# Recurrent scan: the products of keys and values written in other hops of the plan

## The chip, the cores and the metric

One core of one Trainium2 chip. The metric is the time on the device for one execution, in microseconds (us); lower is better. Engines are named as the profile names them: PE is TensorE's matmul side and PEld its weight load, DVE is VectorE, ACT is ScalarE, POOL is GpSimd, and SP is the engine that issues most DMAs.

## The reference, cut to what matters

The program is a two-layer transformer on 256 latent and 256 context tokens of width 1024. Layer 0 mixes tokens with a bidirectional RWKV-7 recurrence, layer 1 with global attention, and feed-forward halves stand around both. The change touches only the recurrence, which is, for each of 16 heads and both directions:

```python
def rwkv_scan(state0, dd, reverse):
    def step(s, inp):
        r_t, w_t, k_t, v_t, a_t, b_t = inp
        sa = jnp.einsum('bhvk,bhk->bhv', s, a_t)
        s = s * w_t[:, :, None, :] + sa[..., None] * b_t[:, :, None, :] + v_t[..., None] * k_t[:, :, None, :]
        return s, jnp.einsum('bhvk,bhk->bhv', s, r_t)
```

Its result goes through a normalization by head, a gain, a bonus term and a gate, and then a projection. The change computes the same numbers.

## The kernel before, in words

The kernel runs its stages one after the other: feed-forward, the projections of the recurrence, `rwkv_scan`, then layer 0's end and layer 1. `rwkv_scan` handles **8 channel tiles** of 128 channels (two heads each). A tile has 8 chunks of 64 tokens in both directions at once, in two halves (hf 0 and 1) of four chunks.

For each tile four generators write its instructions:

- `produce` makes what doesn't depend on the state. A piece is named by a letter and digits. `s` pieces are the scores (four matmuls each, `scp`, L953; DVE masks them into `sc`, L958). `k` pieces transpose the keys of one half and one head (eight transposes, `btp`, L997; ACT copies them to `bkt` one hop later, L999). `v` pieces center the values of one half and one direction (eight matmuls, `vtp`, L977); after the second direction of a half, two ACT copies (L982, L983) put both into `uv` one hop later. So k01 is half 0, head 1, and v10 is half 1, direction 0.
- `solve` inverts small triangular blocks, nearly all on DVE (L1013 to L1035).
- `couple` joins the blocks with 32 by 32 matmuls (`cpl`, L1055, L1076, L1093) and ends with a row of ACT copies into `qt` and `tt` (L1081, L1085, L1098).
- `scan` is the chain. Each chunk takes three **hops**. Hop one: PE `rp` (L1173 and, with the state, L1180), ACT copies it to `rt` (L1184). Hop two: PE `up` from `rt` (L1191), ACT writes `uv` (L1193, L1194). Hop three: PE `sp` (L1200, L1207), ACT writes the new state `S` (L1212). The outputs `yp` (L1155, L1218) stand behind. Each hop needs the ACT copy of the hop before it.

A `readout` runs beside it: a squared copy `sqr` (L1238), small sums `ss` (L1246), and a transposed broadcast `bc` (L1260).

The order is written out by hand: the scheduler is switched off (`manual_schedule`), each engine runs its queue in program order, and `self.plan` says in which hop what is written. The period is P=24 hops: a new tile starts every 24 hops. I count hops 0 to 23 within a period. Tile c's pieces are written in hops 0 to 23 of its own period by `FILL`, `couple` in hops 3 to 16 of the next period, and its chain from hop 17 of that period to hop 16 of the one after. So the **first hop of a tile's chain is hop 17**, and in one period run: the chain of one tile, the couple of the next, the pieces of the one after. Within a hop the chain's part is written first, then what was left over from the hop before (the late copies), couple, the pieces of `FILL`, and the loads. So a piece of hop h stands on PE between the chain's part of hop h and that of hop h+1.

`BK` and `V` say in which hop the loads of the next tile's keys and values are written (SP's queue); they reuse the buffers that the pieces read. The tiles that share PSUM banks (`scp`, `vtp`, `btp`, `cpl`, `ss`, `bc`) rotate over five banks, so a piece that is written elsewhere also reuses another bank. `uv` has four buffers; POOL clears half of each (L971) in the hop of the first value piece of a half, in its queue among the DMAs that load the chain's operands (L929, L933) and the readout's (L1234, L1236).

Of the kernel before, what the change touches and what calls it, by code (L numbers as in the profile page):

```python
# [87 lines left out]
class Net:  # L88


    def __init__(self, ctx, tc, a):
        self.ctx, self.tc, self.nc, self.a = ctx, tc, tc.nc, a
        self.last = {}
        self.plan = dict(
            P=24, SOLVE=14, RATE=5, COUPLE=range(27, 41), SCAN=41,
            FILL={0: ("s000", "s001"), 1: ("s010",), 2: ("s011",), 3: ("s100", "s101"), 4: ("s110",), 5: ("s111",), 7: ("k00",),
                  8: ("k01",), 9: ("v00",), 11: ("v01",), 16: ("k10",), 19: ("k11",), 20: ("v10",), 21: ("v11",)},
            END={(0, 0): (5, (3, 3)), (0, 1): (5, (3, 3)), (1, 0): (5, (3, 3))}, WO=(4, 4), NI=(5, 5),
            FST=(1, 3), WAIT=16, RH=0, FB=16, CLEAR=(14, 18), AS=1, AR=(3, 6), BK=(9, 20), V=(12, 22), LOADS=(30, 42), SS=(6, 18), BC=(10, 22))
        nc = self.nc  # L100
        self.res = ctx.enter_context(tc.tile_pool(name="res", bufs=1))
        self.dram = ctx.enter_context(tc.tile_pool(name="dram", bufs=1, space=DRAM))
        self.vec = self.res.tile([128, NV, KT], F32, name="vec")
        self.cst = self.res.tile([128, NC], F32, name="cst")
        self.ones = self.res.tile([128, 128], F32, name="ones")
        cv = self.res.tile([128, KT, 2], F32, name="cv")
        self.cs = self.res.tile([128, KT, 32], F32, name="cs")
        self.mod = [self.res.tile([128, NMOD, KT, 2], F32, name=f"mod{l}") for l in range(2)]
        self.epsn = self.res.tile([128, 1], F32, name="epsn")
        self.epsg = self.res.tile([128, 1], F32, name="epsg")  # L110
        self.xsp = self.dram.tile([128, 2, KT, CTX], F32, name="xsp")
        nc.sync.dma_start(out=cv, in_=a["cv"])
        nc.sync.dma_start(out=self.vec, in_=a["vec"])
        nc.sync.dma_start(out=self.cst, in_=a["cst"])
        nc.vector.memset(self.epsg, GN_EPS)
        nc.vector.memset(self.ones, 1.0)
        nc.vector.memset(self.epsn, EPS)
        nc.vector.memset(self.cs, 0.0)
        nc.scalar.activation(out=self.cs[:, :, 0:2], in_=cv, func=AF.Silu)
# [19 lines left out]
    def mods01(self, b):  # L139
# [3 lines left out]
        for k4 in range(4):  # L143
            pool = self.first if k4 in self.plan["FST"] else self.wraw
            w = pool.tile([128, 2, 4, 128], F32, tag="mw" if pool is self.first else "raw", name="mw")
# [1473 lines left out]
```

## Time and profile before

| what | us |
|---|---|
| median of 3 runs | 2373.27 |
| the 3 runs | 2365.45, 2373.27, 2374.57 |
| the profiled execution, its own time | 2365.84 |
| its span in the profile | 2363.3 |
| `rwkv_scan` within the span | about 744 to 1116 |
| of that, the chain of the 8 tiles (first `rt` to last `yp`) | 794.9 to 1115 |
| PE busy, share of the span | 93% |
| mean granted TensorE clock | 0.947 |

The profile's times count from the start of the span. A granted clock of 1.00 is 2.4 GHz and 0.50 is 1.2 GHz. The trace counts a matmul of four-byte numbers as two instructions and a transpose as one, so that a value piece is x16 in it and a key piece x8. "busy" of PE counts a matmul to its modelled end; the distance from one start to the next tells better what an instruction costs.

### The profile page before, as it was taken

The page shows a single profiled execution, that of the slowest core. Times are in us where ns is not written, and L with a number is a line of the kernel's source. Part 1 is how long each engine was busy: PE and PEld are TensorE (multiplying, and loading weights), DVE is VectorE, ACT ScalarE, POOL GpSimd, SP SyncE. Part 2 cuts the span into 40 slices and gives each one's busy share as a digit, 9 for nine tenths or more (in the row PEclk, how much of TensorE's full clock was granted, in tenths as well). Part 3 has the DMA queues.
Part 4 walks back from the last instruction along what each step waited for, and adds up shares of the span by engine and source line. Part 5 has one row for each costly group of instructions (what it writes and reads, how often), then busy time and mean ns, then how long its engine had stood idle before and what let it go on. Part 6 is the DMA issues. An engine that isn't in the chain of part 4 may idle for free.

```text
span 2363.3 us, 44881 instructions
## 1 busy us (share of the span) xinstructions
PE 2200.9 (93%) x18548; PEld 1883.3 (80%) x18548; DVE 1516.0 (64%) x2609; ACT 1074.0 (45%) x1912; POOL 153.7 (7%) x222
## 2 busy tenths in 40 slices
PE   6999999887996899998999999999999999998998
PEld 4777889666765778776988788998878898678997
DVE  3798325576897666573788832479983367775554
ACT  3322225455884354454662222464232365554443
POOL 0000000000453122121000000000000000000000
PEclk9999999898998788988999999999999999798999
DMA  7577336442677433322567633567763364103654
GB/s 252 192 219 229 96 103 191 159 134 73 230 245 252 117 99 112 105 85 81 162 210 238 192 93 96 159 195 232 231 205 96 114 178 134 54 17 118 182 180 139
DMA packets 104860, 366.26 MB, mean 155 GB/s; under 512 B 13904, under 2 KB 16208, under 8 KB 101968
## 3 DMA queue, kind: packets, MB, share of 16 engines
q1 hardware_dynamic: 92880, 319.28, 43.2%
q0 software_dynamic: 11776, 44.12, 6.0%
q8 instruction: 145, 2.38, 0.4%
q14 instruction: 59, 0.48, 0.1%
HBM read 330.78 MB, written 32.57 MB: 154 GB/s over the span
## 4 chain that ended last, share of the span: by engine, by line
PE 51%; DVE 10%; ACT 6%; issue 5%; DMA 5%; POOL 1%; DVEq 0%; ACTq 0%; POOLq 0%
PE h L262 6%; PE h L260 5%; PE h L261 5%; PE yps L262 4%; PE yps L260 4%; PE yps L261 4%; DMA y<-in_modt 3%; DVE junk L214 3%; DVE wlo L253 2%; PE scp L953 1%; PE cpl L1055 1%; PE op L1483 1%; PE sp L1207 1%; PE up L1191 1%; PE vtp L977 1%
## 5 line engine op out<-in xcount | busy, mean ns | idle before, releaser
L252 ACT ACTIVATE whi<-wp 128x1024 fp32r<-128x1024 f32 (+1 forms) x396 | 409.3, 1034 | 742.7 <-PE h L261 396.0
L253 DVE TENSOR_TENSOR wlo<-wp,whi 128x1024 fp32r<-128x1024 f32 (+1 forms) x396 | 471.5, 1191 | 385.1 <-ACT whi L252 382.0
L262 PE MATMUL h<-nh,wlo 128*128 128x512 f32 (+1 forms) x1520 | 525.9, 347 | 16.5 <-DVE wlo L253 16.4
L260 PE MATMUL h<-nh,whi 128*128 128x512 f32 (+1 forms) x1520 | 524.5, 346 | 8.4 <-ACT whi L252 6.8
L261 PE MATMUL h<-nh,whi 128*128 128x512 f32 (+1 forms) x1520 | 523.4, 345 | 0.0
L262 PEld LDWEIGHTS h<-nh,wlo 128*128 128x128 f32 x1520 | 290.8, 192 | 59.7 <-DVE wlo L253 26.3
L260 PEld LDWEIGHTS h<-nh,whi 128*128 128x128 f32 x1520 | 291.2, 192 | 42.6 <-ACT whi L252 8.5
L261 PEld LDWEIGHTS h<-nh,whi 128*128 128x128 f32 x1520 | 291.1, 192 | 33.7
L262 PE MATMUL yps<-hid,wlo 128*128 128x256 f32 (+1 forms) x1034 | 314.2, 304 | 1.8 <-DVE wlo L253 1.8
L260 PE MATMUL yps<-hid,whi 128*128 128x256 f32 (+1 forms) x1034 | 314.2, 304 | 0.0
L261 PE MATMUL yps<-hid,whi 128*128 128x256 f32 (+1 forms) x1034 | 313.9, 304 | 0.0
L262 PEld LDWEIGHTS yps<-hid,wlo 128*128 128x128 f32 x1034 | 197.5, 191 | 10.5 <-DVE wlo L253 2.7
L261 PEld LDWEIGHTS yps<-hid,whi 128*128 128x128 f32 x1034 | 197.5, 191 | 7.9
L260 PEld LDWEIGHTS yps<-hid,whi 128*128 128x128 f32 x1034 | 197.5, 191 | 7.9
L214 DVE SCALAR_TENSOR_TENSOR junk<-y 128x1024 bf16<-128x1024 f32 x144 | 175.9, 1222 | 17.9 <-DMA y<-in_modt 15.8
L405 DVE TENSOR_TENSOR gg<-s,h 128x512 f32<-128x512 f32 (+1 forms) x98 | 55.9, 571 | 95.2 <-PE h L262 93.1
L214 DVE SCALAR_TENSOR_TENSOR junk<-dw,cb 128x1024 bf16<-128x1024 f32 x80 | 97.8, 1223 | 13.3 <-DMA dw<-in_modt 9.7
L407 ACT ACTIVATE hid<-gg 128x512 fp32r<-128x512 f32 (+1 forms) x98 | 52.4, 534 | 107.8 <-DVE gg L405 107.6
L262 PE MATMUL pp<-hid,wlo 128*128 128x512 f32 x232 | 92.3, 399 | 6.1 <-DVE wlo L253 6.0
L260 PE MATMUL pp<-hid,whi 128*128 128x512 f32 x232 | 92.6, 399 | 5.0 <-ACT whi L252 5.0
L261 PE MATMUL pp<-hid,whi 128*128 128x512 f32 x232 | 91.5, 395 | 0.0
L953 PE MATMUL scp<-ar,bk 64*128 64x128 f32 x512 | 45.4, 312 | 19.3 <-DVE G L334 11.6
(301 smaller groups left out, 3515.0 us busy)
## 6 DMA issues: line engine op xcount, KB each, us to landing
wp<-in_w SPq DMA_DIRECT2D x243, 512.0 KB, 3.6
wp<-in_w SPq DMA_DIRECT2D x94, 448.0 KB, 3.4
y<-in_modt SPq DMA_DIRECT2D x72, 512.0 KB, 4.4
dw<-in_modt SPq DMA_DIRECT2D x40, 512.0 KB, 4.3
wp<-in_wrkv SPq DMA_DIRECT2D x40, 512.0 KB, 4.0
mw<-in_modw SPq DMA_DIRECT2D x32, 512.0 KB, 5.1
far<-ar POOLq DMA_DIRECT2D x8, 1024.0 KB, 5.8
ar<-far SPq DMA_DIRECT2D x16, 512.0 KB, 4.8
```

Source lines behind the costliest of these rows:

```text
L214: nc.vector.scalar_tensor_tensor(out=junk, in0=ws[i % len(ws)], scalar=1.0, in1=cb[:, s], op0=ALU.mult, op1=ALU.mult, accum_out=self.mod[l ...
L252: nc.scalar.activation(out=hi, in_=raw, func=AF.Copy)
L253: nc.vector.tensor_tensor(out=lo, in0=raw, in1=hi.bitcast(F32), op=ALU.subtract)
L260: nc.tensor.matmul(out=ps, lhsT=wh, rhs=vh, start=first and j == 0, stop=False)
L261: nc.tensor.matmul(out=ps, lhsT=wh, rhs=vl, start=False, stop=False)
L262: nc.tensor.matmul(out=ps, lhsT=wl, rhs=vh, start=False, stop=last and j == n - 1)
L405: nc.vector.tensor_tensor(out=gg, in0=s1, in1=ps[1], op=ALU.mult)
L407: nc.scalar.activation(out=hi, in_=gg, func=AF.Copy)
L953: nc.tensor.matmul(out=p[h][:, c], lhsT=bk[q:q + 64, d, c], rhs=ar[q:q + 64, d, c].rearrange("p s i -> p (s i)"), start=True, stop=True, t ...
L977: nc.tensor.matmul(out=pv[q:q + 64, d, c], lhsT=v[:, d, c], rhs=cst[:, C_CE + q:C_CE + q + 64], start=True, stop=True, tile_position=(0, q))
L1055: nc.tensor.matmul(out=p[hf][q:q + 32, u], lhsT=lhs(8 * hf + u, q), rhs=rhs[q:q + 32, 8 * hf + u], start=True, stop=True, tile_position=(q ...
L1191: nc.tensor.matmul(out=p[w:w + 64, d], lhsT=tt[:, d, c, w:w + 64], rhs=rt[:, d], start=True, stop=True, tile_position=(0, w))
```

## The change

Two lines of the plan. The scores stay in hops 0 to 5. Of keys and values, by hop:

| hop | 7 | 8 | 9 | 11 | 16 | 17 | 19 | 20 | 21 | 23 |
|---|---|---|---|---|---|---|---|---|---|---|
| before | k00 | k01 | v00 | v01 | k10 | | k11 | v10 | v11 | |
| after | k00 | | k01 | | k10 | v10 | v11 | v00 | k11 | v01 |

```diff
             FILL={0: ("s000", "s001"), 1: ("s010",), 2: ("s011",), 3: ("s100", "s101"), 4: ("s110",), 5: ("s111",), 7: ("k00",),
-                  8: ("k01",), 9: ("v00",), 11: ("v01",), 16: ("k10",), 19: ("k11",), 20: ("v10",), 21: ("v11",)},
+                  9: ("k01",), 16: ("k10",), 17: ("v10",), 19: ("v11",), 20: ("v00",), 21: ("k11",), 23: ("v01",)},
-            FST=(1, 3), WAIT=16, RH=0, FB=16, CLEAR=(14, 18), AS=1, AR=(3, 6), BK=(9, 20), V=(12, 22), LOADS=(30, 42), SS=(6, 18), BC=(10, 22))
+            FST=(1, 3), WAIT=16, RH=0, FB=16, CLEAR=(14, 18), AS=1, AR=(3, 6), BK=(10, 22), V=(24, 20), LOADS=(30, 42), SS=(6, 18), BC=(10, 22))
```

The loads move with the pieces that free their buffers: the keys' by one and two hops, the values' of half 0 to the first hop of the next period and of half 1 to hop 20. SP's queue keeps its sequence of keys, values, keys, values.

On PE, hops 8 to 10 of a period (a number of matmuls is given once, as x8; the lines with a sign are what left and what came):

```order
 L1155 MATMUL yp<-r,S 64x64 x4
 L1055 MATMUL cpl<-td,qt 32x32 x16
-L997 MATMUL btp<-cst,bk 128x64 x8
 L1191 MATMUL up<-rt,tt 64x64 x4
 L1055 MATMUL cpl<-td,qt 32x32 x16
-L977 MATMUL vtp<-cst,v 64x64 x8
+L997 MATMUL btp<-cst,bk 128x64 x8
 L1200 MATMUL sp<-S,cst 64x128 x2
 L1207 MATMUL sp<-uv,bkt 64x64 x4
```

The transposes of k01 leave the place ahead of `up` and take that of the values v00 ahead of `sp`; two hops later v01 leaves in the same way.

On PE, hops 16 to 20, where a tile's chain begins:

```order
 L997 MATMUL btp<-cst,bk 128x64 x8
 L1173 MATMUL rp<-uv,sc 64x64 x4
+L977 MATMUL vtp<-cst,v 64x64 x8
 L1191 MATMUL up<-rt,tt 64x64 x4
 L1246 MATMUL ss<-cst,sqr 128x2 x4
 L1207 MATMUL sp<-uv,bkt 64x64 x4
 L1218 MATMUL yp<-sc,uv 64x64 x4
-L997 MATMUL btp<-cst,bk 128x64 x8
+L977 MATMUL vtp<-cst,v 64x64 x8
 L1173 MATMUL rp<-uv,sc 64x64 x4
 L1180 MATMUL rp<-S,ax 64x64 x4
```

The values v10 come between `rp` and `up` of the chain's first hop, and v11 take the place of the keys k11.

On ACT, hops 12 to 14 before (two copies of values, then the state, then couple's copies):

```order
530 L1194 ACTIVATE uv<-up 64x2x64
531 L982 ACTIVATE uv<-vtp 64x8x64
532 L983 ACTIVATE uv<-vtp 64x8x64
533 L1212 ACTIVATE S<-sp,pc 128x64 x2
534 L1081 ACTIVATE qt<-cpl 32x256
535 L1085 ACTIVATE tt<-wd 32x16x32
536 L1184 ACTIVATE rt<-rp 128x128
```

and the same hops after:

```order
530 L1194 ACTIVATE uv<-up 64x2x64
531 L1212 ACTIVATE S<-sp,pc 128x64 x2
532 L1081 ACTIVATE qt<-cpl 32x256
533 L1085 ACTIVATE tt<-wd 32x16x32
534 L1184 ACTIVATE rt<-rp 128x128
```

The two copies have left the place ahead of the state; such pairs now stand behind `rt` of hop 20 and behind `uv` of hop 0.

## Rows read from the trace of the kernel before

Tiles are counted from 0 by their chain. A row of a stretch has its bounds, its length, the busy time of PE, PEld, DVE, ACT and POOL with the number of instructions, the granted clock, the DMA engines' busy share, and GB/s. A row of a timeline has start, duration, engine, line, operation, tiles and shapes, and in brackets the engine's idle time before it and what ended it.

**Rows 1.** The page: granted clock in 40 equal slices, in tenths of full.
```profile
PEclk9999999898998788988999999999999999798999
```

**Rows 2.** Stretches from one chain's first `rt` to the next's (tiles 1, 2, 5).
```profile
835.30:880.80 45.50, 43.06 (x952) 36.54 (x952) 27.51 (x71) 21.36 (x64) 9.17 (x15) 0.81 0.35 102
880.80:922.90 42.10, 40.27 (x952) 34.30 (x952) 27.54 (x71) 21.31 (x64) 9.10 (x15) 0.87 0.37 109
...
1009.60:1050.50 40.90, 38.93 (x952) 33.21 (x952) 27.46 (x71) 21.33 (x64) 9.13 (x15) 0.92 0.23 67
```

**Rows 3.** Timeline of PE, hops 8 to 13 of tile 5's chain: start, us, operation.
```profile
1036.04 0.71 PE L997 MATMUL btp<-cst,bk 64*128 64x64 f32 x8
1036.68 0.45 PE L1191 MATMUL up<-rt,tt 128*64 128x64 f32 x8
...
1037.44 0.69 PE L977 MATMUL vtp<-cst,v 128*64 128x64 f32 x16
1038.06 0.44 PE L1200 MATMUL sp<-S,cst 64*64 64x128 f32 x4
...
1041.39 0.69 PE L977 MATMUL vtp<-cst,v 128*64 128x64 f32 x16
1041.90 0.40 PE L1191 MATMUL up<-rt,tt 128*64 128x64 f32 x8
...
1043.22 0.45 PE L1207 MATMUL sp<-uv,bkt 128*64 128x64 f32 x8
```

**Rows 4.** Timeline of ACT, hops 12 and 13 of the same chain.
```profile
1043.42 0.59 ACT L983 ACTIVATE uv<-vtp 64x512 f32<-64x512 f32 x1
1044.03 0.52 ACT L1212 ACTIVATE S<-sp,pc 128x64 f32<-128x64 f32 x2
```

**Rows 5.** Timeline of all engines, hops 17 and 18, where that chain begins.
```profile
1008.14 0.45 PE L1173 MATMUL rp<-uv,sc 128*64 128x64 f32 x8
...
1009.07 0.60 ACT L1238 ACTIVATE sqr<-yp 128x512 f32<-128x512 f32 x1
...
1009.56 0.27 ACT L1184 ACTIVATE rt<-rp 128x128 f32<-128x128 f32 x1
...
1009.88 0.45 PE L1191 MATMUL up<-rt,tt 128*64 128x64 f32 x8 [1.29 <-ACT rt L1184]
```

**Rows 6.** Stretches of its hops 17, 18 to 21, and 22 to 1.
```profile
1008.10:1010.60 2.50, 1.21 (x21) 0.96 (x19) 2.44 (x4) 2.33 (x7) 1.90 (x4) 0.99 0.32 93
1010.60:1017.40 6.80, 6.80 (x89) 6.32 (x90) 6.12 (x23) 2.04 (x8) 0.00 (x0) 0.50 0.38 130
1017.40:1024.20 6.80, 6.62 (x128) 5.35 (x124) 5.50 (x20) 4.17 (x13) 0.00 (x0) 1.00 0.14 41
```

**Rows 7.** Timeline of PE, its key and value pieces of hops 19 and 20.
```profile
1012.88 1.11 PE L997 MATMUL btp<-cst,bk 64*128 64x64 f32 x8
...
1015.60 1.12 PE L977 MATMUL vtp<-cst,v 128*64 128x64 f32 x16
```

**Rows 8.** Timeline of all engines, its hops 23, 0 and 3.
```profile
1019.89 0.45 PE L1155 MATMUL yp<-r,S 64*64 64x64 f32 x8
1020.19 0.28 ACT L1184 ACTIVATE rt<-rp 128x128 f32<-128x128 f32 x1
...
1020.52 0.45 PE L1191 MATMUL up<-rt,tt 128*64 128x64 f32 x8 [0.18 <-ACT rt L1184]
...
1025.64 1.16 PE L953 MATMUL scp<-ar,bk 64*128 64x128 f32 x16
```

**Rows 9.** DMA: the keys' loads in the scan; their transfers in the whole run.
```profile
bk<-fbk SPq DMA_DIRECT2D x10, 512.0 KB, 3.8
...
DMA to landing us min/median/max: 3.2/5.0/11.5
```

**Rows 10.** Stretches of hops 7 to 10 in tile 1 and 6 to 10 in tile 2.
```profile
860.40:870.60 10.20, 10.20 (x194) 8.53 (x195) 1.82 (x5) 2.83 (x8) 0.00 (x0) 0.50 0.18 56
901.30:911.60 10.30, 10.30 (x328) 8.80 (x330) 4.11 (x9) 4.01 (x13) 1.40 (x3) 1.00 0.57 156
```

## The prediction

> **What bounds the kernel now.** I read the granted clock by slices first, then the scan tile by tile, then the timeline of one period, hop by hop. The clock by slices [rows 1] is full nearly everywhere but in a few slices, and slices 14 to 18, the chain's part of the scan, stand at 8 or 9 tenths. By tile [rows 2] one period takes 40.9 to 45.5 us, and PE is busy in nearly all of it: 38.93 of 40.90 us in tile 5. So the scan is bound by what PE executes, and at which clock, and the chain's hand-overs between PE and ACT are mostly hidden behind other products. Two kinds of places are different.
>
> The first is the chain's beginning. In hop 17 PE ends `rp` at about 1008.5 and then waits 1.29 us for `rt` [rows 5]. ACT is late there, because the tail of `couple` and then `sqr` (0.60 us) stand ahead of `rt` in its queue. In this stretch PE is busy 1.21 of 2.50 us, and then the granted clock falls to 0.50 and stays there for hops 18 to 21 [rows 6]. The same fall stands at this place in each of the tiles 0 to 6. Half clock lasted, from length times twice the missing clock, 40.9 x 2 x 0.08 = 6.5 us in tile 5 and 42.1 x 2 x 0.13 = 10.9 us in tile 2 [rows 2]. What comes before each fall is a wait of PE, and the small sums `ss`.
>
> The second is hops 12 to 16, where ACT's queue holds the chain: the state `S` is ready on PE at 1043.22 + 0.45 = 1043.67 [rows 3] but starts on ACT at 1044.03, behind two copies of values that end at 1044.01 [rows 4].
>
> **The change part by part.** The number of products is the same; only their places move.
>
> *Hops 8, 9 and 11.* In hops 7 to 11 PE runs without idle time at full clock, so what leaves is gained. k01 holds the place from 1036.04 to 1036.68, 0.64 us; v01 from 1041.39 to 1041.90, 0.51 us; in hop 9 k01 takes the place of v00, 0.64 for 1038.06 - 1037.44 = 0.62 us [rows 3]. Together -0.64 - 0.51 + 0.02 = -1.13 us. The chain doesn't show up in their place: `rt` of hop 8 is done before PE would reach `up`, even without k01. This happens in seven periods: six with a chain beside (tiles 0 to 5), and once in the lead-in, where the second tile's pieces run beside the first couple. There PE is at half clock, so the gain lies between nothing and about twice as much; I take the same value. Seven times 1.13 is **-7.9 us**.
>
> *Copies on ACT.* The pair of hop 12 goes, so `S` of hop 13 starts up to 1044.03 - 1043.67 = 0.36 us sooner, and `qt`, `tt` and `rt` behind it too, in a stretch that ACT bounds. Bounds 0 and -0.36; I take -0.3, six times: **-1.8 us**. The pairs now stand behind `rt` in hop 20, where `up` waits for PE's products anyway, and behind `uv` in hop 0, where four score products stand ahead of `sp`. Two copies are 1.2 us [rows 4]; I take both covers to hold, the second narrowly. If it fails, a cost of some 0.2 us a period is my estimate.
>
> *Hop 17.* v10 is 0.51 to 0.62 us on PE and falls into the wait of 1.29 us: **0**. About 0.7 us of wait stay, since ACT's queue isn't shorter. The cover is that queue; without it the cost is 0.6 x 7 = 4 us.
>
> *Hops 19 to 21.* Keys and values change places. At half clock a key piece takes 1.11 and a value piece 1.12 us [rows 7]: **0**, with bounds of 0.2 us either way.
>
> *Hop 23.* `up` waits 0.18 us for `rt` there [rows 8]; v01 in that place costs 0.51 to 0.62 less the 0.18, so 0.33 to 0.44 us, and `rt` comes a little sooner as the pair of copies ahead of it is now one of 0.59 us. I take +0.35 us in seven periods: **+2.4 us**; lower bound +0.1 each.
>
> *Queues.* POOL's clearing of `uv` for half 1 moves ahead of the loads of half 1's operands, and waits there for the last `yp` of hop 16. Those loads start some 4 us later and are needed 12 hops later, so nothing waits. SP's keys load of half 1 starts after k11, that is in hop 21 and not 19, and is first read by the scores of hop 3 at 1025.64 [rows 8]. k11 would now end near 1017.8 (v10's end at 1016.72 [rows 7], and about 1.1 us for `up` and k11), which leaves 7.9 us for a load of 3.8 us [rows 9]: 0.
>
> These terms give -7.9 - 1.8 + 2.4 = **-7.3 us**.
>
> *Clock.* Of a stretch of 6.8 us at half clock, 89 instructions of PE; of the next 6.8 us at full clock, 128 [rows 6]. The same work at full clock would take about 6.8 x 89 / 128 = 4.7 us, so such a stretch costs 2.1 us. The longer ones cost 42.1 - 40.9 = 1.2 us more [rows 2]. Filling the wait in hop 17 takes away half of what comes before each fall, and hop 19 gets 16 instructions in place of 8 in the same time. `ss` and 0.7 us of waiting stay, so I don't expect the falls to go altogether. Bounds: none goes (0), or all (7 x 2.1 + 3 x 1.2 = 18.3 us). I take two of seven falls gone and two of the three long ones shortened: -2 x 2.1 - 2 x 1.2 = **-6.6 us**, nearer to the low end because the row before the fall keeps its second half.
>
> What the keys do to the clock is disputed. Hops 8 to 11 hold at full clock with k01 among them, and the fall of tile 1 in hops 7 to 10 [rows 10] comes after an idle stop of PE that has no releaser. The Trainium skill ("TensorE: Matmul & The Clock Gate", Part 4: PE-mode transpose) says that the full clock doesn't engage for transposes. By that rule k11 in hop 21, where the clock now rises again, speaks against this change; it is a rival below.
>
> *Sum.* -7.3 - 6.6 = -13.9 us. Against the profiled execution that is 2365.84 - 13.9 = 2351.9 us. The four executions shown (three runs and the profiled one) lie in two pairs, about 2365.6 and 2373.9, with the mean at 2369.8, and the median of the runs is in the upper pair. I don't know which pair the next runs fall into, so I set the sum against the mean: 2369.8 - 13.9 = **2355.9 us**.
>
> **The rivals.**
>
> *The clock falls as before.* The product in hop 17 fills a wait but changes no fall. For it: the `ss` of hop 18 stays, and 0.7 us of waiting. Only the PE slots count: 2369.8 - 7.3 = 2362.5 us.
>
> *The falls go altogether.* For it: the fall comes only where PE waits longest. Against: DVE is busy 6.12 of 6.80 us in that stretch [rows 6], so it may come to hold PE. The gain is 7.3 + 18.3, and 4.6 more if tile 1's second fall (45.5 against 40.9 us) goes too: 2369.8 - 30.2 = 2339.6 us.
>
> *The clock rises later.* k11 follows in hop 21 where v11, with twice the instructions, stood. If the rise waits until it is over, each of the seven falls is of the longer kind or 1.2 us longer still: -7.3 + 7 x 1.2 = +1.1, so 2370.9 us. Against: key pieces in hops 7 to 9 run at full clock. This is what the transpose rule named above would do here.
>
> *The keys come late (slower).* SP's load of half 1 has 7.9 us from k11 to the scores of hop 3. The slowest transfer of these tiles took 11.5 us [rows 9]. From 7.9 us on, PE stops in hop 3, for 3.6 us at 11.5: seven times 3.6 is 25.2, less 7.3: 2369.8 + 17.9 = 2387.7 us. For it: the queue is shared with the operands of the chain. Against: the median in the scan is 3.8 us, and the DMA engines are busy 0.14 to 0.38 of these stretches.
>
> **How the numbers follow.** Chances: the forecast 0.50, falls as before 0.23, no falls 0.13, later rise 0.08, late keys 0.06. Half a per cent, about what a measurement of this kernel can tell from no change, is 11.9 us of 2373.27, so faster means under 2361.4 us. The forecast is there but for its weaker end (0.06), the no-falls case wholly, and a little of the falls-as-before case (0.03): 0.44 + 0.13 + 0.03 = 0.60 faster. Slower is the late-keys case: 0.06. Same is the rest, 0.34. The range leaves out late keys, the top of the later rise and the strongest half of the no-falls case: 2338 to 2370 us, which also holds both pairs of executions for the forecast.
>
> **What would show it.** Right: in hop 17, `vtp` between `rp` and `up`, and `up`'s wait about 0.7 us and not 1.29; `up` of hop 9 some 0.64 us sooner after `past` (`yp`, L1155) of hop 8; no pair of copies ahead of `S` in hop 13; tiles of 39 to 40 us where the clock falls once, near 37 where it doesn't. Wrong: periods that stay at 40.9 us or more with the slots moved; half clock over hops 22 and 23; waits of `scp` for the keys' DMA in hop 3; a wait of `scp` of hop 1 for the copies of hop 0.

## The result, and the profile after

The changed kernel takes 2355.93 us (median of 8 runs, 2342.77 to 2360.99) against 2371.95 us for the kernel before (8 runs beside it). The medians differ by 16.0 us, where the forecast was 13.9 us. The ratio of the means is 0.9926, with a 95% interval of 0.9902 to 0.9951, so the changed kernel is 0.74% faster by the means. The profiled execution took 2342.77 us, the shortest of the eight, and its span is 2340.7 us with a mean granted clock of 0.955. It is 22.6 us shorter than the span before. From the first score product of the scan to the chain's first `rt` it has 39.3 us in place of 40.3, the chain itself (from that `rt` to the start of its last `yp`) 299.2 in place of 319.0, and what comes behind the chain 1247.0 in place of 1249.4.

The granted clock by slices of the kernel after, from its page. Slices 14 to 18 are to be set beside [rows 1].

```profile
PEclk9999999898998799998999999999999999798999
```

The stretches of four tiles of the kernel after (tiles 1 to 4), with the columns of [rows 2]:

```profile
833.00:872.30 39.30, 36.17 (x952) 30.60 (x952) 27.36 (x71) 21.27 (x63) 9.17 (x15) 1.00 0.41 117
872.30:910.40 38.10, 35.73 (x952) 30.36 (x952) 27.34 (x71) 21.24 (x63) 9.15 (x15) 1.00 0.41 121
910.40:950.10 39.70, 37.59 (x952) 31.96 (x952) 27.28 (x71) 21.43 (x63) 9.12 (x15) 0.96 0.41 116
950.10:993.60 43.50, 40.01 (x952) 33.81 (x952) 27.34 (x71) 21.24 (x63) 9.15 (x15) 0.88 0.36 106
```

Tiles 1 and 2 keep the full clock throughout, which no tile of [rows 2] does. Tile 3 has one fall of 3.4 us at the chain's beginning and takes 39.7 us. Of the 1.6 us that it takes more than tile 2, 1.5 lie in hops 6 to 10 (10.8 us against 9.3), where PE stops for 0.80 and 0.26 us; the fall itself costs 0.1 us. Tile 4 keeps the clock at the beginning and loses it in hops 7 to 10.

The timeline of PE after, hops 17 to 22 at the beginning of tile 5's chain, as [rows 5 to 7] had it:

```profile
992.21 0.45 PE L1173 MATMUL rp<-uv,sc 128*64 128x64 f32 x8
992.50 0.64 PE L977 MATMUL vtp<-cst,v 128*64 128x64 f32 x16
993.96 0.45 PE L1191 MATMUL up<-rt,tt 128*64 128x64 f32 x8 [0.82 <-ACT rt L1184]
994.34 1.05 PE L1246 MATMUL ss<-cst,sqr 128*128 128x2 f32 x8
995.32 0.45 PE L1207 MATMUL sp<-uv,bkt 128*64 128x64 f32 x8
...
998.10 0.71 PE L997 MATMUL btp<-cst,bk 64*128 64x64 f32 x8
998.74 0.44 PE L1200 MATMUL sp<-S,cst 64*64 64x128 f32 x4
...
1001.07 0.79 PE L1260 MATMUL bc<-cst,rb 128*128 128x128 f32 x4 [1.28 <-ACT rb L1254]
1001.79 0.70 PE L1173 MATMUL rp<-uv,sc 128*64 128x64 f32 x8
```

The values v10 stand between `rp` and `up`, and `up` waits 0.82 us for `rt`, not 1.29. The clock now holds through hops 17 to 21: `sp` takes 0.45 us, and the key piece in hop 21 holds its place for 998.74 - 998.10 = 0.64 us. But there is a **new wait**: `bc` of hop 22 stands 1.28 us for `rb`. Right behind it the clock falls here (`rp` takes 0.70 us). The reason for the wait is on DVE, whose timeline at the same time reads:

```profile
1000.02 0.23 DVE L1027 TENSOR_TENSOR wi<-wi,tl 128x63 f32<-128x63 f32 x1
1000.16 0.20 DVE L1251 RECIPROCAL rs<-rs 128x8 f32<-128x8 f32 x1
1000.28 0.22 DVE L1023 TENSOR_TENSOR tl<-xl,wi 128x64 f32<-128x64 f32 x1
```

The reciprocal `rs`, from which ACT makes `rb`, stands in DVE's queue among the short steps of `solve`, which run one behind the other from 995.32 to past it. In the kernel before, with PE at half clock in hops 18 to 21, no `bc` of hop 22 waits for `rb`; with PE at full clock PE arrives first. In all three profiled executions of the changed kernel `bc` waits in just those of the tiles 1 to 6 that have no fall in hops 17 to 21.

Hops 8 and 9 of that chain on PE, beside [rows 3]:

```profile
1019.31 0.45 PE L1155 MATMUL yp<-r,S 64*64 64x64 f32 x8
1019.69 0.45 PE L1055 MATMUL cpl<-td,qt 32*32 32x32 f32 x32
1020.08 0.45 PE L1191 MATMUL up<-rt,tt 128*64 128x64 f32 x8
...
1020.84 0.71 PE L997 MATMUL btp<-cst,bk 64*128 64x64 f32 x8
1021.48 0.44 PE L1200 MATMUL sp<-S,cst 64*64 64x128 f32 x4
```

There is no key piece ahead of `up`, and no wait in its place. On ACT, in hop 13, the state is no longer behind copies but waits for PE itself [rows 4]:

```profile
1025.60 0.27 ACT L1194 ACTIVATE uv<-up 64x128 f32<-64x128 f32 x1
1026.74 0.52 ACT L1212 ACTIVATE S<-sp,pc 128x64 f32<-128x64 f32 x2 [0.86 <-PE sp L1207]
```

The fall of tile 4 comes behind a stop of PE in hop 6. On PE, and then the stretches of hops 2 to 6 and 7 to 10:

```profile
969.87 0.31 PE L1055 MATMUL cpl<-tn,sc 32*32 32x32 f32 x12
971.30 0.38 PE L1055 MATMUL cpl<-tn,sc 32*32 32x32 f32 x20 [1.12 <-issue]
971.60 1.05 PE L1246 MATMUL ss<-cst,sqr 128*128 128x2 f32 x8
```
```profile
964.00:972.00 8.00, 6.88 (x192) 5.72 (x190) 6.23 (x11) 2.37 (x8) 4.31 (x7) 1.00 0.83 218
971.00:981.50 10.50, 10.20 (x216) 8.66 (x218) 1.40 (x4) 2.50 (x8) 0.00 (x0) 0.65 0.17 57
```

The stop lies in the middle of a group of like matmuls, after 12 of 32 instructions, and no semaphore ends it ("issue"). The DMA engines are 0.83 busy in this stretch. The small sums `ss` follow, as they do at the chain's beginning, and then the clock is at half for most of hops 7 to 10. The kernel before has a stop and such a fall in tile 1 [rows 10].

### The profile page after: what moved, and what is told of

The parts are those of the page before. It is cut to its first block, busy times and chain, and to the rows that moved or that the text cites. A ratio compares the mean times of both kernels' runs of the same rounds, so it can differ in the third digit from the quotient of the medians.

```text
span 2340.7 us, 44866 instructions
## 1 busy us (share of the span) xinstructions
PE 2178.6 (93%) x18548; PEld 1862.8 (80%) x18548; DVE 1515.9 (65%) x2609; ACT 1073.9 (46%) x1912; POOL 153.7 (7%) x222
## 4 chain that ended last, share of the span: by engine, by line
PE 51%; DVE 11%; issue 5%; ACT 5%; DMA 5%; POOL 1%; DVEq 0%; ACTq 0%; POOLq 0%
PE h L262 6%; PE h L260 5%; PE h L261 5%; PE yps L262 4%; PE yps L260 4%; PE yps L261 4%; DMA y<-in_modt 3%; DVE wlo L253 2%; DVE junk L214 2%; PE scp L953 1%; PE cpl L1055 1%; PE op L1483 1%; DMA fgl<-yx 1%; PE yo L262 1%; PE yo L261 1%
## 5 line engine op out<-in xcount | busy, mean ns | idle before, releaser
L262 PE MATMUL h<-nh,wlo 128*128 128x512 f32 (+1 forms) x1520 | 525.3, 347 | 17.3 <-DVE wlo L253 17.1
L405 DVE TENSOR_TENSOR gg<-s,h 128x512 f32<-128x512 f32 (+1 forms) x98 | 55.9, 571 | 93.8 <-PE h L262 91.7
```

Of the source, the lines that this page charges most:

```text
L262: nc.tensor.matmul(out=ps, lhsT=wl, rhs=vh, start=False, stop=last and j == n - 1)
L405: nc.vector.tensor_tensor(out=gg, in0=s1, in1=ps[1], op=ALU.mult)
```

## The experiments

In every diff a line with - is the line of the changed kernel (for the first experiment of the kernel before), cut to what differs. The table takes one profiled execution of each kernel, adds the stretches of tiles 0 to 5 by hops from one operation of the chain on ACT to the next, and gives behind the slash the time in it at half clock (length times twice the missing clock). Where the text counts falls at the chain's beginning, it counts the tiles 1 to 6, because the clock of tile 0 still depends on the lead-in.

| kernel | hops 17 to 21 | 22, 23 | 0 to 5 | 6 to 10 | 11 to 16 | sum |
|---|---|---|---|---|---|---|
| before | 56.8 / 50.4 | 14.8 / 0.4 | 59.5 / 0 | 65.2 / 10.2 | 59.3 / 1.1 | 255.6 |
| after | 44.4 / 9.0 | 17.0 / 3.4 | 59.2 / 0 | 64.0 / 10.2 | 54.1 / 0 | 238.7 |
| after, second execution | 46.7 / 17.9 | 19.5 / 9.0 | 59.2 / 0 | 72.3 / 32.6 | 55.0 / 2.8 | 252.8 |
| after, third execution | 44.4 / 8.9 | 18.5 / 6.8 | 59.2 / 0 | 68.1 / 20.5 | 54.2 / 0 | 244.4 |
| hop 17 alone | 50.0 / 36.3 | 14.7 / 0 | 59.5 / 0 | 65.8 / 13.7 | 58.6 / 7.4 | 248.5 |
| all but hop 17 | 55.3 / 41.3 | 16.4 / 1.9 | 59.2 / 0 | 72.1 / 33.6 | 54.4 / 0.5 | 257.3 |
| v10 doubled | 44.0 / 3.8 | 17.1 / 3.4 | 59.2 / 0 | 71.8 / 30.7 | 54.1 / 0 | 246.2 |
| keys in hop 19 | 52.3 / 28.7 | 15.1 / 0.1 | 59.2 / 0 | 62.4 / 6.8 | 54.3 / 2.8 | 243.3 |
| `bc` later | 44.6 / 12.6 | 14.4 / 0 | 58.9 / 0 | 68.4 / 23.9 | 54.4 / 0 | 240.7 |
| `bc` later, again | 44.0 / 11.1 | 14.4 / 0 | 59.0 / 0 | 62.3 / 9.6 | 55.5 / 0.6 | 235.1 |
| `ss` in hop 8 | 49.0 / 18.0 | 15.6 / 0 | 59.2 / 0 | 63.8 / 12.6 | 58.1 / 1.1 | 245.6 |
| both of these | 47.9 / 19.1 | 14.3 / 0 | 59.0 / 0 | 69.1 / 29.6 | 62.3 / 15.7 | 252.5 |
| scores' loads later | 50.9 / 31.1 | 16.9 / 3.4 | 59.2 / 0 | 55.9 / 0 | 62.9 / 12.2 | 245.8 |
| and `bc` later | 51.8 / 33.2 | 15.8 / 2.1 | 58.8 / 0 | 56.7 / 0 | 62.3 / 15.6 | 245.5 |

What differs between rows of one kernel shows how much a single execution says: only differences that are larger than those between the three executions of the changed kernel are used.

**The changed kernel again** (no edit), with its runs beside the next three experiments.

> The changed kernel once more, beside the others on the same chip. Theory A (the gain is 7 us of PE slots and the rest fewer clock falls at the chain's beginning, and how many falls an execution has varies from run to run): the ratio to before is again 0.990 to 0.995, the single times spread by 10 us or more, and a profile whose time is near 2356 us shows more half clock in the scan than the 37.5 us of the profile of 2342.8 us: some 50 to 70 us. Rival B (the slots alone, the clock is chance): the half clock of the scan is as far from that of before (88.7 us) as chance has it, and the ratio is nearer to 0.997.

Measured: 2349.18 us, ratio 0.9919 (0.9891 to 0.9947). The gain is repeated. The profiled execution was one of the longer ones (2359.4 us), and its row in the table says where from: hops 6 to 10 at half clock for 32.6 us. The whole chain has 76 us at half clock against 33 in the first profile, so more, as theory A had it, and above its 50 to 70.

**Hop 17 alone:** in the kernel before, only v10 moves, from hop 20 into hop 17.

```diff
-..., 16: ("k10",), 19: ("k11",), 20: ("v10",), 21: ("v11",)},
+..., 16: ("k10",), 17: ("v10",), 19: ("k11",), 21: ("v11",)},
```

> The kernel before with one piece moved: v10 from hop 20 to hop 17, into the wait of the chain's first hop. Everything else, loads too, as before. Theory A: hop 20 gets 0.5 us shorter (0.9 at half clock) and the falls become fewer or shorter: -3.6 us of slots and -5 to -10 us of clock, ratio 0.994 to 0.996. Rival B: the slot alone, -3.6 to -6 us, ratio 0.9975 to 0.9985, with falls at the beginning of every chain as before.

Measured: 2358.74 us, ratio 0.9954 (0.9935 to 0.9973). This alone is faster than before. Its beginning of tile 3's chain:

```profile
916.96 0.93 PE L997 MATMUL btp<-cst,bk 64*128 64x64 f32 x8
917.83 0.69 PE L1173 MATMUL rp<-uv,sc 128*64 128x64 f32 x8
918.30 1.07 PE L977 MATMUL vtp<-cst,v 128*64 128x64 f32 x16
919.34 0.69 PE L1191 MATMUL up<-rt,tt 128*64 128x64 f32 x8
```

In tiles 1, 2, 3 and 6 the clock has fallen before hop 17, in the key piece of hop 16 (`rp` takes 0.69 us, not 0.45), and `up` waits for nothing, since PE is slow enough. In tile 4 it doesn't fall at the beginning, and in tile 5 late and for 3.4 us. So the piece in hop 17 helps where the clock is still full, and in four of six tiles something ahead of it had already acted; hops 11 to 16 are still those of the kernel before there (58.6 us against 54.1). What makes the clock fall in hop 16 was not isolated. The ratio lies where theory A put it; in those four tiles the falls are those of rival B.

**All but hop 17:** in the changed kernel v10 goes on to hop 18.

```diff
-..., 16: ("k10",), 17: ("v10",), 19: ("v11",), ...
+..., 16: ("k10",), 18: ("v10",), 19: ("v11",), ...
```

> The changed kernel with v10 written in hop 18 in place of hop 17, behind the small sums; the first hop of the chain is again without an independent product. Theory A: the wait for rt is 1.3 us again, hop 18 costs 0.5 us more, and the falls come back in every tile: 8 to 15 us slower than the changed kernel, ratio to before 0.997 to 1.000. Rival B: only the slot counts, 7 x 0.5 = 3.6 us slower than the changed kernel, ratio to before 0.994 to 0.995.

Measured: 2358.69 us, ratio 0.9949 (0.9925 to 0.9974). The timeline of PE at the beginning of tile 3's chain:

```profile
913.95 0.45 PE L1173 MATMUL rp<-uv,sc 128*64 128x64 f32 x8
915.69 0.45 PE L1191 MATMUL up<-rt,tt 128*64 128x64 f32 x8 [1.29 <-ACT rt L1184]
915.97 0.64 PE L977 MATMUL vtp<-cst,v 128*64 128x64 f32 x16
916.54 1.87 PE L1246 MATMUL ss<-cst,sqr 128*128 128x2 f32 x8
918.34 0.70 PE L1207 MATMUL sp<-uv,bkt 128*64 128x64 f32 x8
```

The wait of 1.29 us is back, and with it a fall in each of the tiles 1 to 6 (in the table 41.3 us at half clock against 8.9 to 17.9). Each of the six begins 0.2 to 1.2 us after that wait has ended; in the three executions of the changed kernel 5 of 18 tiles fall. The same product one place further on, after the wait, does not help. In the traces this is the clearest verdict of the study: leaving hop 17 without a product brings the falls back. Filling it is not enough by itself, as the kernel with hop 17 alone shows. The time says less: the median is 9.5 us above that of the changed kernel beside it, as theory A had it, but the ratio lies in rival B's range and the two intervals overlap.

**v10 doubled:** every matmul of v10 is issued twice, so that it fills the rest of the wait.

```diff
-                    for c in range(4):
+                    for c in [c for c in range(4) for _ in range(2 if (hf, d) == (1, 0) else 1)]:
```

> The changed kernel with every matmul of v10 issued twice (the same values into the same place), so hop 17 has 1.1 us of products in place of 0.55 in its wait of 1.4 us, and 56 matmuls more in all. Theory A: the added work costs nothing and the falls become rarer still: 3 to 8 us faster than the changed kernel, half clock in the scan 40 us or less in any run. Rival B: no gain; 0 to 3 us slower. If it is faster though it does more, the clock is what moved it.

Measured: 2358.37 us, ratio 0.9949 (0.9928 to 0.9970). At tile 5's beginning, PE:

```profile
1000.72 1.10 PE L977 MATMUL vtp<-cst,v 128*64 128x64 f32 x32
1002.18 0.45 PE L1191 MATMUL up<-rt,tt 128*64 128x64 f32 x8 [0.36 <-ACT rt L1184]
...
1009.30 0.66 PE L1260 MATMUL bc<-cst,rb 128*128 128x128 f32 x4 [1.29 <-ACT rb L1254]
```

With 0.36 us of wait left, none of the tiles 1 to 6 falls in hops 17 to 21, in this one execution. (There are 64 matmuls more in all, not 56.) The time that was expected from it didn't come, and both theories missed: the median is 9.2 us above that of the changed kernel beside it, with intervals that overlap. `bc` now waits in all six tiles, and four tiles fall in hops 7 to 10. This points away from the beginning and to those two places.

**Keys in hop 19:** in the changed kernel the rest of the sequence becomes k11, v11, v00, with hop 17 as it is (the load of the values follows by one hop).

```diff
-..., 19: ("v11",), 20: ("v00",), 21: ("k11",), 23: ("v01",)},
+..., 19: ("k11",), 20: ("v11",), 21: ("v00",), 23: ("v01",)},
```

> The changed kernel with the keys k11 back in hop 19, ahead of the values v11 (hop 20) and v00 (hop 21); hops 7 to 17 and 23 as in the change, and the load of half 1's values one hop later. PE has the same products. Theory A (what stands in hops 17 to 19 decides the falls): the falls at the chain's beginning come back in about four of the tiles 1 to 6, as in the kernel with the first hop alone, and the ratio to before is 0.994 to 0.997, 3 to 8 us slower than the changed kernel. Rival B (only hop 17 matters): falls in two tiles at most, as in the changed kernel, ratio 0.991 to 0.994.

Measured: 2358.28 us, ratio 0.9977 (0.9956 to 0.9998), between a quarter and a half of the gain. The changed kernel did not run beside this kernel and the next three; they are set against it by the ratio to the kernel before. PE at the beginning of tile 2's chain, and of tile 6's:

```profile
874.83 0.45 PE L1191 MATMUL up<-rt,tt 128*64 128x64 f32 x8 [0.82 <-ACT rt L1184]
875.21 1.05 PE L1246 MATMUL ss<-cst,sqr 128*128 128x2 f32 x8
...
876.81 0.98 PE L997 MATMUL btp<-cst,bk 64*128 64x64 f32 x8
877.71 0.69 PE L1173 MATMUL rp<-uv,sc 128*64 128x64 f32 x8
```
```profile
1037.50 0.70 PE L1173 MATMUL rp<-uv,sc 128*64 128x64 f32 x8
```

Everything up to the key piece is as in the changed kernel; in tile 2 the clock falls in the key piece, and in tile 1 at its start. Five of the six tiles fall in hops 17 to 21 (28.7 us in the table), as theory A had it. But in three of the five the clock has fallen before the key piece, where the program is that of the changed kernel: in tiles 4 and 6 `rp` of hop 17 already takes 0.70 us, and in tile 5 it falls in `ss`. So only two falls can come from what stands in hop 19, and that it matters is likely, not shown. Whether it would be because keys are transposes or because a key piece is 8 instructions and a value piece 16 in the same time, this run does not tell.

**`bc` later:** `bc` goes from hop 22 to 23 and v01 takes its place in hop 22.

```diff
-..., 21: ("k11",), 23: ("v01",)},   ... BC=(10, 22)
+..., 21: ("k11",), 22: ("v01",)},   ... BC=(10, 23)
```

> The changed kernel with bc and v01 exchanged: the values v01 in hop 22, the transposed broadcast in hop 23. Theory A (where the clock stays full, bc of hop 22 waits 1.28 us for rb, which waits for DVE): the wait in hop 22 goes in the tiles without a fall, 4 x 1.2 = 4 to 5 us faster than the changed kernel, and falls in hops 22 and 23 no longer occur, another 1 to 3 us; ratio to before 0.988 to 0.992. Rival B: DVE is the bound, the wait only moves to bc in hop 23 or to the scores of hops 1 to 3, 0 to 1 us faster.

Measured: 2344.85 us, ratio 0.9915 (0.9882 to 0.9947). PE at tile 5's beginning:

```profile
1000.65 0.54 PE L1180 MATMUL rp<-S,ax 128*64 128x64 f32 x8 [0.78 <-ACT S L1212]
...
1001.50 0.66 PE L1260 MATMUL bc<-cst,rb 128*128 128x128 f32 x4
```

`bc` waits no more, and the falls in hops 22 and 23 are gone (14.4 us against 17.0 to 19.5). Most of the wait has only changed its name: ACT still stands with `rb`, waiting for DVE, and the state `S` is behind it in ACT's queue, so that `rp` waits 0.78 us. The ratio is the one of theory A; the wait that moves is the one of rival B.

**`ss` in hop 8** (and `bc` of half 0 in hop 12), to part the small sums from the stop in hops 6 and 7; and **both of these** together.

```diff
-SS=(6, 18), BC=(10, 22)
+SS=(8, 18), BC=(12, 22)
```

> The changed kernel with the readout's small sums of half 0 moved from hop 6 to hop 8, which the change emptied, and its bc from hop 10 to hop 12. Nothing else moves. Theory A (falls in hops 7 to 10 come when an idle stop of PE without a releaser meets the small sums of hop 6): the stops in hops 6 and 7 stay, about 1 us each in the same tiles, but falls in hops 7 to 10 become none or one: 5 to 9 us faster than the changed kernel in an execution like the second profile of it, ratio to before 0.986 to 0.991. Rival B: the stop alone makes the fall; the falls stay at one to four, ratio 0.991 to 0.995.

> Both: v01 in hop 22 and bc in hop 23, small sums of half 0 in hop 8 and its bc in hop 12. Theory A: the gains add, 9 to 15 us faster than the changed kernel, ratio to before 0.984 to 0.989. Rival B: 0 to 2 us.

Measured: 2358.75 us, ratio 0.9980 (0.9955 to 1.0005), and 2354.22 us, ratio 0.9962 (0.9944 to 0.9980). A miss: without `ss` beside them the stops became longer, up to 2.0 us, falls stayed in two and in four of the tiles 0 to 5, hops 11 to 16 grew by 4 and 8 us, and hops 17 to 21 were longer too (49.0 and 47.9 us against 44.4 to 46.7). Sums in another hop than the stop do not take these falls away.

**Scores' loads later:** the operand of the scores (`ar`, two loads of 512 KB on SP's queue) is loaded in hops 17 and 19 and not 3 and 6, away from the other loads; alone, and **with `bc` later**. The changed kernel and `bc` later ran once more beside them. (One more line lets a load be written before its tile's other pieces; it adds no instruction.)

```diff
-AR=(3, 6)
+AR=(17, 19)
```

> The changed kernel once more, so that the three kernels beside it are compared with it on one chip. Both theories: ratio to before 0.990 to 0.995; in its profile falls at the chain's beginning in two tiles or fewer, and one to three falls in hops 7 to 10, each in a tile where PE stops in hop 6 or 7 without a releaser.

> The kernel with bc in hop 23 and v01 in hop 22 again, beside the changed kernel. Theory A (the wait of bc for rb was PE time that is now used): 3 to 6 us faster than the changed kernel of this call, so a ratio to before of 0.988 to 0.992. Rival B (its lower median of the last call, against a ratio like the changed kernel's, was the chip): the same as the changed kernel within 2 us.

> The changed kernel with the loads of the next tile's score operands (ar, two of 512 KB) written in hops 17 and 19 in place of 3 and 6, away from the operand and readout loads of POOL. Theory A (the stops of PE without a releaser in hops 6 and 7 are instruction fetches held up by these loads: DMA engines are busy 0.83 of hops 2 to 6 there): the stops of 0.7 to 1.3 us in hops 6 and 7 go or shrink under 0.4 us, the falls in hops 7 to 10 with them, 3 to 8 us faster than the changed kernel. Rival B (the stops come from the number of instructions alone): they stay where they are, and the time stays within 2 us.

> Both: bc in hop 23, v01 in hop 22, and the loads of ar in hops 17 and 19. Theory A: the gains add, 7 to 13 us faster than the changed kernel, ratio to before 0.985 to 0.990. Rival B: as e5 alone.

Measured: the changed kernel 2351.72 us, ratio 0.9948 (0.9922 to 0.9974); `bc` later 2347.48, 0.9917 (0.9889 to 0.9945); loads later 2355.74, 0.9948 (0.9931 to 0.9966); with both 2351.50, 0.9936 (0.9914 to 0.9958). With the loads later, the timeline of PE has these rows in hop 14 of two tiles:

```profile
868.68 0.63 PE L1093 MATMUL cpl<-wd,qt 32*32 32x32 f32 x27 [2.26 <-issue]
950.61 0.47 PE L1093 MATMUL cpl<-wd,qt 32*32 32x32 f32 x17 [2.62 <-issue]
```

The stops of hops 6 and 7 went from tiles 1, 3 and 4, and with them every fall in hops 6 to 10, in both kernels (55.9 and 56.7 us against 64.0 to 72.3). But stops of 2.3 to 2.6 us in one kernel and 1.2 to 3.0 us in the other appeared in hops 13 and 14 of the same tiles, with falls behind all of them but one, and all of it was given back: hops 11 to 16 take 62.9 and 62.3 us against 54.1 to 55.0, some of the falls last into the next chain's beginning (50.9 and 51.8 us against 44.4 to 46.7), and the lead-in takes 42.2 and 43.2 us against 38.6 to 39.3. So the gain of theory A did not come, though its falls went. The stops hang on when these loads run, and most falls of hops 7 to 10 on the stops; not every stop is followed by a fall.

The packets in the traces say what PE waits for. The DMA queue 8, whose packets the trace calls "instruction", moves 16 KB at a time. Over all 14 traces, each of the 83 stops of PE in the chain that are longer than 0.2 us and have no semaphore behind them ends 1.2 to 1.6 us after such a packet has landed; times that lie so behind a packet make up 7.5% of the chain. For the stop above that ends at 971.30, the packet ran from 968.61 to 969.84. So, as far as the traces show, PE stops for instructions that arrive late. The packets themselves are not slow there (0.9 to 1.5 us each, as elsewhere); that the loads make them start late fits the move of the stops and is not shown.

**The best version** is `bc` later: 0.9915 and 0.9917 of the time before. Measured side by side, its median was 4.2 us below the changed kernel's, but the intervals overlap, so that is probable and not settled.

## Why the prediction was right, step by step

**Hops 8, 9 and 11.** Right. In tiles without a fall hop 8 takes 1.08 us in place of 1.72, so 0.64 less as said; hop 11 takes 1.08 in place of 1.54, 0.46 where 0.51 was said; hop 9 takes 1.83 in place of 1.81. The lead-in took 1.0 us less, for a term of 1.1, and 1.7 and 1.4 less in the two other executions; since PE also waits for loads of keys there, this does not show that term by itself.

**Copies on ACT.** Right: hop 12, with the start of hop 13's `S` at its end, takes 1.43 us in place of 1.68, 0.25 for a term of 0.3. In the tiles 0 to 5 both covers held: `scp` of hop 1 doesn't wait, and hops 0 to 5 take 59.2 us in place of 59.5. In tile 6 no scores of a further tile stand there, and the second cover failed, a case that the prediction doesn't have: on ACT the two copies run from 1043.74 to 1044.92, `S` only behind them, and PE waits for it:

```profile
1045.32 0.54 PE L1180 MATMUL rp<-S,ax 128*64 128x64 f32 x8 [0.52 <-ACT S L1212]
```

**Hop 17.** The wait that stays is 0.82 us, where about 0.7 was said, and v10 costs nothing.

**Hop 23.** 1.16 us in place of 0.83: +0.33 for a term of 0.35. With six tiles the slots add up to 6 x (-0.64 - 0.46 + 0.02 - 0.25 + 0.33) = -6.0 us. With the lead-in's -1.0 and, in tile 6, hop 23's +0.33 and hop 0's +0.52 it is some -6.2, where -7.3 was said.

**Queues.** Right: no `scp` of the chain's periods waits for its keys, in any of the three profiled executions, so the late keys were no danger. Waits for keys there are in the lead-in only, where the kernel before has one too.

**Clock.** The sum was right, its parts were not. First a reading: that a wait and `ss` come before each fall holds in tiles 1, 5 and 6 of the kernel before, where the clock falls while `ss` runs. In tiles 2 and 4 it falls within the wait, ahead of `ss`, and in tile 3 in the last 0.1 us of `rp`, so that it is at half for the whole wait:

```profile
921.91:923.20 1.29, 0.00 (x2) 0.00 (x1) 1.26 (x3) 1.27 (x4) 1.29 (x3) 0.50 0.34 108
```

So `ss` is not what those falls need. At the chain's beginning the effect is far greater than the two of seven falls that I allowed: of the tiles 1 to 6 all fall there before, and two, two and one in the three profiled executions of the changed kernel. Hops 17 to 21 gain 10.1 to 12.4 us in six tiles, and this with the new wait of `bc` already in it. The step that was too small was to take half of a wait for half of its effect: with 0.82 us left most falls go, with 0.36 (one execution) all of them. The kernel with hop 17 empty bears out that the product in the wait does it. What a fall costs was mis-sized as well. Hops 17 to 21 of tile 2, without a fall, and of tile 3, with one of 3.4 us:

```profile
872.32:879.64 7.32, 5.84 (x124) 5.17 (x124) 6.67 (x22) 4.33 (x15) 0.47 (x1) 1.00 0.41 131
910.41:917.80 7.39, 7.06 (x122) 6.44 (x124) 6.74 (x22) 4.50 (x14) 0.47 (x1) 0.77 0.30 93
```

The short fall costs 0.1 us, because without it `rb` waits for DVE, which is busy 6.67 of 7.32 us. Such are three of the five falls that are left; the falls before, of 6.8 and 10.2 us, made these hops 9.0 to 10.2 us long. Then two things that I had not put into the sum took part of it back. One is `bc`: in four, four and five of the tiles 1 to 6 it waits about 1.28 us, and hops 22 and 23 lose 2.2 to 4.7 us in all where +2.1 was the price of v01. I had it in the rival without falls as a warning (DVE busy 6.12 of 6.80 us), but without a price, and put a tile without a fall near 37 us; it takes 38.1. The other is hops 6 to 10: they should be 3.7 us shorter, and are 1.2 shorter in one execution and 7.1 and 2.9 longer in the others, each with one to three falls there. Over the three executions the tiles 0 to 5 take 245.3 us in the mean, 10.3 less than in the profiled one of the kernel before; without the 6.0 of the slots that leaves about 4.3 for the clock with the new wait and the stops in it, against 5.7 predicted for six of the seven falls if the 6.6 is shared evenly.

So a part of the agreement is luck: the falls at the beginning were underrated, and what would be late next was left unpriced. Whether more falls in hops 6 to 10 are a consequence of the change, or only what these executions happened to have, stays open. The stops behind them are there before as well (0.43 us in tile 1, 1.23 in tile 4), the changed kernel varies between 2342.77 and 2369.56 us from run to run, and of the kernel before one execution was profiled.

**The rivals.** Falls as before: excluded by the trace. No falls: not seen, but its doubt, that DVE comes to hold PE, came true. Later rise: not seen as a rule. In the rows of hops 17 to 22 above, the key piece of hop 21 runs at full clock, and in four of the five falls the clock is back before it. In the fifth (tile 2 of the second execution, a fall of 10.2 us) the key piece takes 1.11 us and the clock rises 3.4 us behind it. Half clock in hops 22 and 23, which was to be a sign of being wrong, did come in six more tiles, each time behind the wait of `bc`. The Trainium skill ("TensorE: Matmul & The Clock Gate", Part 4: PE-mode transpose) says that the full clock doesn't engage for transposes. The 0.64 us of that key piece, at a granted clock of 1.00, disagree with it as it is put; whether transposes alone would hold the clock up, no run here shows. Some falls do begin in a key piece (hop 16 in four tiles with hop 17 alone, hop 19 in tile 2 with the keys there), others in `rp`, in `ss` or in a value piece.

## What to carry to other kernels

A wait of one microsecond that looks harmless can cost more in what the clock does afterwards than by its length (here 1.7 to 2.9 us for a wait of 1.29): look at the granted clock of the next few microseconds before calling it hidden. In these traces filling the wait itself took falls away, and the same product one place later did not. A fall costs only what PE would otherwise have gained: where another engine is next in line, a short one is nearly free. Before crediting the full gain, name and price what arrives late once the engine is fast: here a reciprocal in DVE's queue, and instructions that reach PE late while loads run.

## What the hardware showed that I had not expected

- PE stops for 0.4 to 3.0 us in the middle of a group of like matmuls, with no semaphore behind it, and goes on 1.2 to 1.6 us after a packet of instructions has landed. In hops 6 and 7 this happens in mostly the same tiles from kernel to kernel, beside DMA engines that are 0.83 busy, and it moves to hops 13 and 14 when two loads per tile move.
- One program spreads over 20 us and more (2343.24 to 2363.49 in 7 runs, 2343.27 to 2369.56 in 12 others). In the profiled executions the difference lies where the clock falls: the chain takes 299.2 us in one and 315.7 in another, and the third, of 2366.99 us, has its scan begin 15 us later than the first. A difference of 4 us between two versions is not settled by a dozen runs.
- A fall in hops 6 to 10, with its stop, costs 5.4 us (tile 4 with 43.5 us against 38.1 for tile 2). One of 3.4 us in hops 22 and 23 costs 1.4 us (4.1 us in tile 5 against 2.7), and a fall just as long at the chain's beginning 0.1 us.
